# Both gates of a hybrid layer in the seven-product form, with weights summed and split once, ahead of time

## The chip, the cores and the metric

The kernel runs on one core of a Trainium2 chip. The metric is the device time of one execution in microseconds (us); of several runs the median is taken. TensorE (PE) does the matrix products, VectorE (DVE) and ScalarE (ACT) the element-wise work, GpSimd (POOL) a little, and SyncE (SP) issues nearly all transfers (DMAs), all from one queue that is worked off in order.

## The reference

One layer, D = 1024 channels, T = 2048 tokens, float32. What matters here is the frame around the mixer and its last two lines:

```python
def hybrid_layer(x, p_i, ...):
    h = rmsnorm(x, norm_pre)
    proj = h @ w_in
    # ... convolutions, chunked state-space scan (SSD), gates z -> y_ssd, y_sc
    mix = jnp.concatenate([y_ssd, y_sc], axis=-1) @ w_out
    x = x + rmsnorm(mix, norm_post)

    gate = jax.nn.sigmoid(x @ w_ple_gate)
    return x + gate * (p_i @ w_ple_proj)
```

The change concerns `x @ w_ple_gate`, a product of 2048 x 1024 by 1024 x 1024, called the gate below. The sigmoid is computed as half of 1 + tanh(half).

## The kernel before

**Numbers in two parts.** Every operand of a product is split into a high part (a cast on ACT to fp32r) and the remainder (a subtraction on DVE), and a product takes three matmuls (`PASSES`): high by high, high by low, low by high. `split_w` does it for a weight piece of 128 x 512 (four blocks of 128 x 128), `split_act` for an activation of 128 x 512 (L209 and L210 in the profile). One matmul is 128 x 128 by 128 x 512.

**Weights.** `Weights` holds the sequence of all weight pieces of the program in the order of their use. `W.next()` hands out the next one and starts the fetch of those that fit into six slots of 512 KB (`pw`, tag `wsp`, names `ws_...`). `direct` fetches a piece: a 256 KB load (L140) into one of nine raw buffers (`praw`, names `wr_...`), then the cast (L144) and the subtraction (L145) into the slot.

**Stages.** Channels are rows of 128, tokens are taken in groups of 512 (`tg` 0 to 3).

- Stage A, 0 to 1033 us: two blocks of 1024 tokens, the second one from 545 us. Each multiplies by `w_in` in 13 groups of two or one tiles, in a seven-product form: for a 2 x 2 arrangement of blocks, seven products of sums and differences of the blocks replace eight products (`Wino.multiply`, L316). The weight sums for it are made on DVE from raw pieces (`wino_pieces`, L184, L185, L187, L193). `multiply` takes a generator `meanwhile` and steps it after each of the seven products.
- The SSD scan to 1306 us, with half of the output projection under it.
- The rest of the output projection, `out_proj(0)` and `out_proj(2)` (products `mo`), to 1494.5 us; its results are the tiles `x2`.
- The gates. `gate_plain(0)` handles token groups 0 and 1: for each of 8 output rows and 2 groups, 24 matmuls `mg` (L220), 384 in all, with 16 raw pieces of `w_g`. `gate_seven(2)` handles groups 2 and 3: 28 pieces of 12 matmuls `mg_X`, `mg_Y` (L1259), 336 in all, in the order `GATES`; piece `(p, n)` is product p for output row pair n. Products 1, 5 and 6 are copied out of their bank, the others go to `finish` (tanh on ACT, three operations on DVE at most, a store).

**Order of the work.** All stages after the scan step through units (one unit is one `yield`): units 0 to 31 are the output projection, then 16 units of the plain gate and 28 of the other. `plan` says after which unit other work is written down: the norm of a token group (`second`, `norm`), the residual (`residual`, L1151 and L1152, with loads `xres`), the operands' split (`operands`, `operand`), the sums of gate weights (`gate_sums`: 16 loads, 16 sums, 16 stores to `sg_d`, L1192 to L1200), and the copy of `x2` into DRAM (`kept`), since `operand` overwrites it in groups 2 and 3; `finish` loads it again (`x<-x_d`). A scheduler turns the written order into each engine's order.

Of the kernel before, what the change touches and what calls it, by code (L numbers as in the profile page):

```python
# [64 lines left out]
def hybrid_kernel(ctx: ExitStack, tc: tile.TileContext, xT, pT, w_t, w_dt, w_o, w_g, w_p, cols_d, cst_d, outT):  # L65
# [1023 lines left out]
    with ExitStack() as st:  # L1089
# [64 lines left out]
        def operands(tg, d):  # L1154

            for i in range(2):
                sp_.setdefault(tg, []).append(split_act(x2s_[tg][d + i], f"x2s_{tg}_{d + i}", FIRST[2 * (tg % 2) + d // 4]))

        def gate_plain(t):

            for dp in range(0, KD, 2):
                sp = []
                for tg in (t, t + 1):
                    banks = pss.tile([P, 2, TG], F32, tag="ssd", name=f"mg_{tg}_{dp}")
                    for i in range(2):
                        d, ts_, ps = dp + i, slice(tg * TG, (tg + 1) * TG), banks[:, i, :]
                        pe = pp.tile([P, TG], F32, tag="pe", name=f"pe_{tg}_{d}")
                        nc.sync.dma_start(pe, ple_d[tg * TG // TB][d, :, tg * TG % TB:tg * TG % TB + TG])
                        for q in range(2):
                            if tg == t:  # L1170
                                sp.append(W.next(len(sp)))
                            mm3([(ps, sp[2 * i + q], sp_[tg])], 4 * q, 4, KD)
                        th = pp.tile([P, TG], F32, tag="gth", name=f"gth_{tg}_{d}")
                        S.activation(th, ps, AF.Tanh, scale=0.5)
                        V.scalar_tensor_tensor(th, th, 1.0, pe, ALU.add, ALU.mult)
                        V.scalar_tensor_tensor(th, th, 0.5, x2s_[tg][d], ALU.mult, ALU.add)
                        nc.sync.dma_start(outT[d, :, ts_], th)
                        yield

        def tmp(name):  # L1180
            return pp.tile([P, TG], F32, tag="x2", name=name, bufs=NG * KD)

        def kept(tg, d):
            for i in range(2):
                nc.sync.dma_start(x2_d[tg][d + i], x2s_[tg][d + i])

        def gate_sums(n):

            w = []
            for i, h in ((0, 0), (0, 1), (1, 0), (1, 1)):  # L1190
                w.append(tmp(f"sg_{n}_{i}{h}"))
                nc.sync.dma_start(w[-1].rearrange("p (k c) -> p k c", c=P), w_g[n + 4 * i, :, 4 * h:4 * h + 4, :])  # L1192
            yield
            a, b, c, d = w
            V.tensor_tensor(d, c, d, ALU.add)
            V.tensor_tensor(c, c, a, ALU.subtract)
            V.tensor_tensor(a, a, d, ALU.subtract)
            V.tensor_tensor(b, b, a, ALU.add)
            for i, v in enumerate((d, a, c, b)):
                nc.sync.dma_start(sg_d[n][i], v.rearrange("p (k c) -> p k c", c=P))  # L1200
            yield

        ops_ = {}

        def operand(g, k):

            p, t = GORDER[g], NG - 2
            b11, b12, b21, b22 = x2s_[t][k], x2s_[t + 1][k], x2s_[t][4 + k], x2s_[t + 1][4 + k]
            if p == 6:
# [4 lines left out]
            elif p == 7:
                src = b12
                V.tensor_tensor(b12, b12, b22, ALU.subtract)
            else:
                src = {1: b11, 2: b21, 5: b11, 3: b22, 4: b21}[p]
            ops_.setdefault(p, []).append(split_act(src, f"x2s_{p}{k}", FIRST[g % 4]))

        def gate_seven(t):
# [21 lines left out]
            for m, (p, n) in enumerate(GATES):  # L1243
                if m + 2 < len(GATES) and GATES[m + 2][1] % 2 == 0 and at(*GATES[m + 2]):
                    L.begin("pe", *at(*GATES[m + 2]))
                    L3.begin("x2", *at(*GATES[m + 2]))
# [10 lines left out]
                for k in range(4):  # L1257
                    for q, (a, b) in enumerate(PASSES):
                        TE.matmul(out, sp[:, a, k, :], ops_[p][k][:, b, :], start=p in OPENS and k == 0 and q == 0,  # L1259
# [36 lines left out]
        second(0, 16, (19, 20, 21, 22))  # L1296
        second(1, 18, (24, 25, 26, 27))
        for tg, units in ((0, (29, 29, 30, 30)), (1, (31, 31, 32, 32))):
            for n, u in enumerate(units):
                after(u, lambda tg=tg, d=2 * n: operands(tg, d))  # L1300
        second(2, 32, (34, 35, 36, 37))
        second(3, 34, (38, 39, 40, 41))
        for n in range(4):
            sums = gate_sums(n)
            for u in (36, 38):
                after(u + 2 * n, lambda sums=sums: next(sums))
        operands_at(0, 45, 46)
        operands_at(1, 46, 47)
        operands_at(2, 48, 49, 50, 51)
        operands_at(3, 52, 53)  # L1310
        operands_at(4, 54, 55)
        operands_at(5, 57, 59)
        operands_at(6, 61, 63)
# [70 lines left out]
```

## Time and profile before

| | us |
|---|---|
| three runs | 1675.41, 1677.62, 1675.29 |
| their median | 1675.41 |
| profiled execution | 1674.55 |
| its span | 1672.8 |
| granted TensorE clock, mean over the span | 0.997 of full speed |
| end of the output projection in it | 1494.5 |
| end of the last gate matmul in it | 1667.4 |

The span is the time from the first to the last instruction that the profiler saw; the execution's own time has 1.75 us around it. "Busy" is time in which an engine worked on an instruction. In the windows, each row gives a stretch, its length, the busy time of PE, PE's weight loads (PEld), DVE, ACT and POOL with the number of instructions, then the granted clock, the mean busy share of the 16 DMA engines and the rate in GB/s. In the waits, a row gives who waited for whom, the sum, the number of times and the longest. In the chain, a row is a piece of the path that ended last: start, length, engine and line. A row of the DMA issues gives the number of transfers, the size of one and the median time from issue to landing.

### The profile page before, as it was taken

Reading aid. Unit: us, or ns where it says so; the run is one execution under the profiler, and the core shown is the slowest. Engines: PE = TensorE matmul, PEld = TensorE weight load, DVE = VectorE, ACT = ScalarE, POOL = GpSimd, SP = SyncE. Lnnn points to the kernel's source line nnn. Section 1 sums busy time; section 2 is a strip of 40 time slices with the busy share of each in tenths; the row PEclk is TensorE's granted clock in tenths of the full one; section 3 lists DMA queues with packets and bytes.
Section 4 is the critical chain, followed back from the end, with each engine's and each line's share of the span. In section 5 each row is a group of like instructions: output and inputs, shape, how many; then the busy total and the mean of one; then the engine's idle time right before and its main releaser. Section 6 shows DMA issues by size and latency. Waiting matters only on the chain.

```text
span 1672.8 us, 22881 instructions
## 1 busy us (share of the span) xinstructions
PE 1647.1 (98%) x8352; PEld 1350.9 (81%) x8352; DVE 1278.3 (76%) x1909; ACT 800.0 (48%) x1442; POOL 45.6 (3%) x79
## 2 busy tenths in 40 slices
PE   9999999999999999999999999999999899999998
PEld 7888888888888888888888888877778688888776
DVE  5997777988669877677877677679878738768696
ACT  7763444434337434343444354566665424253363
POOL 0000000000000100100000001000000000000000
PEclk9999999999999999999999999999999999999999
DMA  8452322773226313221322237888888736537974
GB/s 300 160 195 80 100 95 77 260 252 110 65 65 218 134 64 109 77 82 63 107 70 103 69 102 245 257 297 273 283 299 249 251 110 208 194 118 264 307 259 151
DMA packets 132228, 281.15 MB, mean 168 GB/s; under 512 B 17930, under 2 KB 19466, under 8 KB 131092
## 3 DMA queue, kind: packets, MB, share of 16 engines
q1 hardware_dynamic: 132116, 279.70, 50.3%
q8 instruction: 65, 1.06, 0.3%
q14 instruction: 47, 0.39, 0.1%
HBM read 202.93 MB, written 76.72 MB: 167 GB/s over the span
## 4 chain that ended last, share of the span: by engine, by line
PE 87%; DMA 5%; DVE 4%; ACT 2%; issue 1%; SPq 1%; DVEq 0%; ACTq 0%
PE mo L220 9%; PE os L779 6%; PE mg L220 3%; PE mg_X L1259 3%; PE A_ple L220 3%; PE mg_Y L1259 2%; DMA mraw<-yz_d 2%; PE A_xs1X L316 1%; PE A_gc0X L316 1%; PE A_gc6X L316 1%; PE A_gb7X L316 1%; PE A_gb5X L316 1%; PE A_gc7X L316 1%; PE A_z3X L316 1%; PE A_xs3X L316 1%; PE A_gb6X L316 1%
## 5 line engine op out<-in xcount | busy, mean ns | idle before, releaser
L779 PE MATMUL os<-act_m,ws_os 128*128 128x512 f32 x768 | 184.3, 396 | 1.0 <-ACT A_z L714 0.7
L220 PE MATMUL mo<-act_m,ws_o 128*128 128x512 f32 x768 | 180.9, 394 | 4.5 <-DVE x L1115 1.8
L220 PEld LDWEIGHTS mo<-act_m,ws_o 128*128 128x128 f32 x768 | 142.6, 188 | 41.3 <-DVE x L1115 4.9
L779 PEld LDWEIGHTS os<-act_m,ws_os 128*128 128x128 f32 x768 | 142.2, 189 | 35.5 <-issue 4.6
L220 PE MATMUL mg<-act_x2s,ws_g 128*128 128x512 f32 x384 | 90.4, 394 | 3.3 <-ACT ws_g L144 3.3
L145 DVE TENSOR_TENSOR ws_A_gb<-wr_A_gb,ws_A_gb 128x512 fp32r<-128x512 f32 x96 | 66.0, 687 | 35.6 <-ACT ws_A_gb L144 35.5
L220 PEld LDWEIGHTS mg<-act_x2s,ws_g 128*128 128x128 f32 x384 | 71.3, 188 | 20.8 <-ACT ws_g L144 3.7
L144 ACT CAST ws_A_gc<-wr_A_gc 128x512 fp32r<-128x512 f32 x96 | 59.8, 623 | 57.8 <-PE A_gc5X L316 8.3
L144 ACT CAST ws_A_gb<-wr_A_gb 128x512 fp32r<-128x512 f32 x96 | 59.6, 621 | 54.8 <-PE A_cb0Y L316 4.3
L990 ACT ACTIVATE m<-m,adt 128x128 f32<-128x128 f32 x256 | 78.2, 391 | 7.9 <-DMA m<-acs_d 7.8
L633 DVE SCALAR_TENSOR_TENSOR xo<-ux,cols,xo 128x1024 f32<-128x1024 f32 x60 | 76.7, 1281 | 5.9 <-ACT xo L629 4.8
L145 DVE TENSOR_TENSOR ws_A_gc<-wr_A_gc,ws_A_gc 128x512 fp32r<-128x512 f32 x96 | 66.1, 688 | 14.4 <-ACT ws_A_gc L144 13.1
L209 ACT CAST act_m<-mraw 128x512 fp32r<-128x512 f32 x64 | 38.1, 621 | 31.7 <-DVE mraw L836 18.7
L144 ACT CAST ws_A_xs<-wr_A_xs 128x512 fp32r<-128x512 f32 x48 | 29.9, 622 | 44.7 <-issue 11.6
L993 DVE SCALAR_TENSOR_TENSOR m<-m,gsb 128x1024 f32<-128x1024 f32 x32 | 39.1, 1247 | 14.9 <-ACT m L990 13.3
L144 ACT CAST ws_A_z<-wr_A_z 128x512 fp32r<-128x512 f32 x48 | 29.9, 622 | 42.0 <-DVE wr_A_z L193 10.2
L145 DVE TENSOR_TENSOR ws_A_z<-wr_A_z,ws_A_z 128x512 fp32r<-128x512 f32 x48 | 33.0, 687 | 22.1 <-ACT ws_A_z L144 22.1
L220 PE MATMUL A_ple<-act_p,ws_p 128*128 128x512 f32 x192 | 48.3, 409 | 1.5 <-ACT act_p L209 1.0
L1115 DVE TENSOR_TENSOR x<-mo,part 128x512 f32<-128x512 f32 x32 | 22.0, 689 | 35.2 <-PE mo L220 33.9
L210 DVE TENSOR_TENSOR act_m<-mraw,act_m 128x512 fp32r<-128x512 f32 x64 | 41.8, 685 | 6.7 <-ACT act_m L209 6.4
L1259 PE MATMUL mg_X<-act_x2s,ws_g 128*128 128x512 f32 x192 | 45.6, 393 | 0.7 <-ACT gth L1230 0.7
L220 PEld LDWEIGHTS A_ple<-act_p,ws_p 128*128 128x128 f32 x192 | 36.7, 194 | 11.7 <-ACT act_p L209 1.9
(533 smaller groups left out, 3750.1 us busy)
## 6 DMA issues: line engine op xcount, KB each, us to landing
wr_A_gc<-in_w_t_dram SPq DMA_DIRECT2D x64, 256.0 KB, 2.6
wr_A_gb<-in_w_t_dram SPq DMA_DIRECT2D x64, 256.0 KB, 3.2
m<-acs_d SPq DMA_DIRECT2D x32, 512.0 KB, 8.3
ple_d<-A_pe SPq DMA_DIRECT2D x32, 256.0 KB, 3.5
wr_A_xs<-in_w_t_dram SPq DMA_DIRECT2D x32, 256.0 KB, 2.7
ysc_d<-vs SPq DMA_DIRECT2D x16, 512.0 KB, 2.7
wr_A_z<-in_w_t_dram SPq DMA_DIRECT2D x32, 256.0 KB, 2.6
xs_d<-xo SPq DMA_DIRECT2D x16, 512.0 KB, 2.8
```

The lines of the kernel that those rows point to most:

```text
L144: S.copy(sp[:, 0, :kn, :], raw[:, :kn, :])
L145: V.tensor_tensor(sp[:, 1, :kn, :], raw[:, :kn, :], sp[:, 0, :kn, :].bitcast(F32), ALU.subtract)
L209: S.copy(a[:, 0, :], src)
L210: V.tensor_tensor(a[:, 1, :], src, a[:, 0, :].bitcast(F32), ALU.subtract)
L220: TE.matmul(out, sp[:, a, (k0 + k) % 4, :], act[k0 + k][:, b, :], start=k0 + k == 0 and q == 0, stop=k0 + k == n - 1 and q == 2)
L316: TE.matmul(out, sp[:, a, k % 4, :], t[:, b, ts_], start=p in OPENS and k == 0 and q == 0, stop=k == nk - 1 and q == 2, skip_group_check=True)
L633: V.scalar_tensor_tensor(o, u[:, q:q + TB], col(w0 + q), o, ALU.mult, ALU.add)
L779: inst = f(*a, **k)
L990: S.activation(m[:, c, :], m[:, c, :], AF.Exp, bias=nacs[b][:, h, c:c + 1])
L993: V.scalar_tensor_tensor(mf, mf, 1.0, s["gsb"][gr], ALU.min, ALU.mult)
L1115: V.tensor_tensor(x2[d], ps[:, i, :], pt[:, i, :], ALU.add)
L1259: TE.matmul(out, sp[:, a, k, :], ops_[p][k][:, b, :], start=p in OPENS and k == 0 and q == 0, stop=k == 3 and q == 2, skip_group_check=True)
```

## The change

`gate_plain`, `operands`, `kept` and `gate_sums` go. `gate_weights` makes, for each of the four output row pairs n, all seven weight operands: four loads of 256 KB from `w_g`, four sums or differences, seven casts and seven subtractions, and seven stores of 512 KB (high and low part) into `sg_d[n]`. It runs as `meanwhile` of the second block of stage A, in groups 1 to 7 but the one that holds `cb`, up to seven steps after the seven products of a group. Both gates are `gate_seven`, for t = 0 and t = 2. Their weights come by `stored`: one 512 KB load from `sg_d` into the slot, with no cast and no subtraction. `operand` no longer overwrites `x2`: sums go to tiles of the raw pool `praw`, and `finish` reads `x2` where it is. The plan has other units, and `norm` a `lag` between its two steps.

```diff
-    sg_d = [dram.tile([4, P, 4, P], F32, name=f"sg_d{n}") for n in range(KD // 2)]
-    x2_d = {g: dram.tile([KD, P, TG], F32, name=f"x2_d{g}") for g in range(NG // 2, NG)}
+    sg_d = [dram.tile([7, P, 2, TG], F32, name=f"sg_d{n}") for n in range(KD // 2)]
...
+    def stored(src, name):
+
+        return name, lambda sp: nc.sync.dma_start(sp.bitcast(F32).rearrange("p a k c -> p a (k c)"), src)
...
-    seq += [direct(w_g[d, :, 4 * q:4 * q + 4, :], f"g0_{d}_{q}", praw) for d in range(KD) for q in (0, 1)]
...
-    seq += [direct(gate_piece(p, n), f"g2_{p}_{n}", praw) for p, n in GATES]
+    for t in range(0, NG, 2):
+        seq += [stored(sg_d[n][p - 1], f"g{t}_{p}_{n}") for p, n in GATES]
...
+        def gate_weights():
+
+            def loads(n):
+                w = []
+                for i, h in ((0, 0), (0, 1), (1, 1), (1, 0)):
+                    w.append(A.ph.tile([P, TG], F32, tag="h2", name=f"A_g{n}_{i}{h}"))
+                    nc.sync.dma_start(w[-1].rearrange("p (k c) -> p k c", c=P), w_g[n + 4 * i, :, 4 * h:4 * h + 4, :])
+                return w
+
+            for n in range(KD // 2):
+                a, b, d, c = loads(n)
+                yield
+                for p, src, op in ((1, a, None), (2, b, None), (4, d, None), (5, d, (c, d, ALU.add)),
+                                   (7, c, (c, a, ALU.subtract)), (6, a, (a, d, ALU.subtract)), (3, b, (b, a, ALU.add))):
+                    if op:
+                        V.tensor_tensor(src, *op)
+                    t = A.ph.tile([P, 2, TG], F32R, tag="h1", name=f"A_gs{n}_{p}")
+                    S.copy(t[:, 0, :], src)
+                    V.tensor_tensor(t[:, 1, :], src, t[:, 0, :].bitcast(F32), ALU.subtract)
+                    nc.sync.dma_start(sg_d[n][p - 1], t.bitcast(F32))
+                    yield
...
+            elif b and 0 < n < 8 and ("cb", 0) not in prs:
+                mean = (next(gw, None) for _ in range(7))
...
+            new = lambda: praw.tile([P, 4, P], F32, tag="wraw", name=f"t{p}_{t}{k}").rearrange("p k c -> p (k c)")
             if p == 6:
-                src = tmp(f"t2_{k}")
-                V.tensor_tensor(b11, b12, b11, ALU.subtract)
-                V.tensor_tensor(src, b11, b22, ALU.subtract)
-                V.tensor_tensor(b21, b21, src, ALU.add)
+                sums_[5, k] = new()
+                V.tensor_tensor(sums_[5, k], b12, b11, ALU.subtract)
+                src = sums_[6, k] = new()
+                V.tensor_tensor(src, sums_[5, k], b22, ALU.subtract)
...
-                V.scalar_tensor_tensor(th, th, 0.5, L3.get("x2", tg, d - i)[:, i, :], ALU.mult, ALU.add)
+                V.scalar_tensor_tensor(th, th, 0.5, x2s_[tg][d], ALU.mult, ALU.add)
...
-        for stage, t in ((out_proj, 0), (out_proj, 2), (gate_plain, 0), (gate_seven, 2)):
+        for stage, t in ((out_proj, 0), (out_proj, 2), (gate_seven, 0), (gate_seven, 2)):
```

What moves is seen in three places. In the rows below stand the line in the code, the operation, output and inputs, the shape, and how many stand together. On PE the order is the same up to the first gate matmul. There, before, right behind the output projection (names: `mg_0_0` is the bank of group 0, row 0; `ws_g0_0_1` the raw piece of row 0, half 1):

```order
L220 MATMUL mg_0_0_12674<-act_x2s_0_4_12621,ws_g0_0_1_12514 128x512 x3
L220 MATMUL mg_0_0_12674<-act_x2s_0_5_12624,ws_g0_0_1_12514 128x512 x3
L220 MATMUL mg_0_0_12674<-act_x2s_0_6_12627,ws_g0_0_1_12514 128x512 x3
L220 MATMUL mg_0_0_12674<-act_x2s_0_7_12630,ws_g0_0_1_12514 128x512 x3
L1131 MATMUL pn2_2_12738<-ones_d_102,ssq2_2_11974 128x1 x4
L220 MATMUL mg_1_0_12784<-act_x2s_1_0_12662,ws_g0_0_0_12509 128x512 x3
```

And now, at the same place of PE (`mg_0_X0` is the bank pair X of row pairs 0 and 1, `ws_g0_1_1` product 1 of row pair 1, `act_x2s_0_12` operand 1, part 2, of gate 0):

```order
L1236 MATMUL mg_0_X0_12814<-act_x2s_0_12_12767,ws_g0_1_0_12667 128x512 x3
L1236 MATMUL mg_0_X0_12814<-act_x2s_0_13_12770,ws_g0_1_0_12667 128x512 x3
L1151 MATMUL pn2_2_12847<-ones_d_100,ssq2_2_12132 128x1 x4
L1236 MATMUL mg_0_X2_12884<-act_x2s_0_10_12729,ws_g0_1_2_12815 128x512 x3
L1236 MATMUL mg_0_X0_12814<-act_x2s_0_10_12729,ws_g0_1_1_12669 128x512 x3
L1236 MATMUL mg_0_X0_12814<-act_x2s_0_11_12732,ws_g0_1_1_12669 128x512 x3
```

A piece is now used for 12 matmuls in a row, where one piece of before served 24, in two token groups.

On DVE, in the first group of stage A's second block, before (`ws_A1_gc0_3_0` is a split weight piece, product 3, of tile gc0 in block 1):

```order
L193 TENSOR_TENSOR wr_A1_gb0_000_4612<-wr_A1_gb0_010_4784,wr_A1_gb0_000_4612 128x512
L145 TENSOR_TENSOR ws_A1_gc0_3_0_4762<-wr_A1_gc0_000_4574,ws_A1_gc0_3_0_4762 128x512
L145 TENSOR_TENSOR ws_A1_gb0_3_0_4783<-wr_A1_gb0_000_4612,ws_A1_gb0_3_0_4783 128x512
L145 TENSOR_TENSOR ws_A1_gc0_7_0_4804<-wr_A1_gc0_100_4631,ws_A1_gc0_7_0_4804 128x512
L145 TENSOR_TENSOR ws_A1_gb0_7_0_4821<-wr_A1_gb0_100_4671,ws_A1_gb0_7_0_4821 128x512
L145 TENSOR_TENSOR ws_A1_gc0_2_0_4838<-wr_A1_gc0_010_4763,ws_A1_gc0_2_0_4838 128x512
L145 TENSOR_TENSOR ws_A1_gb0_2_0_4855<-wr_A1_gb0_010_4784,ws_A1_gb0_2_0_4855 128x512
```

And now (`A_gs0_1` is the split gate weight of product 1, row pair 0; `A_g0_11` a raw block of it):

```order
L196 TENSOR_TENSOR wr_A1_gb0_000_4610<-wr_A1_gb0_010_4782,wr_A1_gb0_000_4610 128x512
L549 TENSOR_TENSOR A_gs0_1_5108<-A_g0_00_5061,A_gs0_1_5108 128x512
L144 TENSOR_TENSOR ws_A1_gc0_3_0_4760<-wr_A1_gc0_000_4572,ws_A1_gc0_3_0_4760 128x512
L144 TENSOR_TENSOR ws_A1_gb0_3_0_4781<-wr_A1_gb0_000_4610,ws_A1_gb0_3_0_4781 128x512
L144 TENSOR_TENSOR ws_A1_gc0_7_0_4802<-wr_A1_gc0_100_4629,ws_A1_gc0_7_0_4802 128x512
L144 TENSOR_TENSOR ws_A1_gb0_7_0_4819<-wr_A1_gb0_100_4669,ws_A1_gb0_7_0_4819 128x512
L144 TENSOR_TENSOR ws_A1_gc0_2_0_4836<-wr_A1_gc0_010_4761,ws_A1_gc0_2_0_4836 128x512
L549 TENSOR_TENSOR A_gs0_2_5146<-A_g0_01_5063,A_gs0_2_5146 128x512
L549 TENSOR_TENSOR A_gs0_4_5182<-A_g0_11_5065,A_gs0_4_5182 128x512
L144 TENSOR_TENSOR ws_A1_gb0_2_0_4853<-wr_A1_gb0_010_4782,ws_A1_gb0_2_0_4853 128x512
L546 TENSOR_TENSOR A_g0_11_5065<-A_g0_10_5067,A_g0_11_5065 128x512
```

All 44 added operations of DVE stand in its rows 671 to 809, mixed with the splits, sums and evacuations of the block's first groups.

On SP's queue in the first gate, before (`wr_g...` raw pieces, `sg...` the weight sums, `pe` the embedding's projection):

```order
L1200 DMA sg_d2_94<-sg_2_01_13146 128x512
L1192 DMA sg_3_00_13231<-in_w_g_dram 128x512
L1192 DMA sg_3_01_13233<-in_w_g_dram 128x512
L1192 DMA sg_3_10_13235<-in_w_g_dram 128x512
L1192 DMA sg_3_11_13237<-in_w_g_dram 128x512
L1168 DMA pe_1_5_13239<-ple_d0_84 128x512
L1168 DMA pe_0_6_13271<-ple_d0_84 128x512
L140 DMA wr_g0_7_1_13279<-in_w_g_dram 128x512
```

And now, around the load of piece 5_2 (product 5, row pair 2):

```order
L151 DMA ws_g0_5_1_13058<-sg_d1_93 128x1024
L151 DMA ws_g0_3_0_13077<-sg_d0_92 128x1024
L1215 DMA out_0_dram<-kp_0_13_12929 128x512
L151 DMA ws_g0_3_1_13099<-sg_d1_93 128x1024
L840 DMA xres_3_2_13191<-in_xT_dram 128x2x512
L151 DMA ws_g0_5_2_13120<-sg_d2_94 128x1024
L840 DMA xres_3_4_13244<-in_xT_dram 128x2x512
L151 DMA ws_g0_5_3_13150<-sg_d3_95 128x1024
L151 DMA ws_g0_3_2_13171<-sg_d2_94 128x1024
```

The sums' loads and stores are gone from there; a weight is one transfer twice as large. On PE now, where 5_2 is used (`ws_g0_6_3` is the piece ahead of it in the written order, `mg_0_Y52` its bank):

```order
L1236 MATMUL mg_0_Y5_13149<-act_x2s_0_50_12844,ws_g0_5_0_13030 128x512 x3
L1236 MATMUL mg_0_Y5_13149<-act_x2s_0_51_12879,ws_g0_5_0_13030 128x512
L1236 MATMUL mg_0_X2_12884<-act_x2s_0_60_12841,ws_g0_6_3_13003 128x512 x3
L1236 MATMUL mg_0_X2_12884<-act_x2s_0_61_12876,ws_g0_6_3_13003 128x512 x3
L1236 MATMUL mg_0_X2_12884<-act_x2s_0_62_12905,ws_g0_6_3_13003 128x512 x3
L1236 MATMUL mg_0_X2_12884<-act_x2s_0_63_12935,ws_g0_6_3_13003 128x512 x3
L1236 MATMUL mg_0_Y5_13149<-act_x2s_0_51_12879,ws_g0_5_0_13030 128x512 x2
L1236 MATMUL mg_0_Y5_13149<-act_x2s_0_52_12908,ws_g0_5_0_13030 128x512 x3
L1236 MATMUL mg_0_Y5_13149<-act_x2s_0_53_12938,ws_g0_5_0_13030 128x512 x3
L1236 MATMUL mg_0_Y52_13248<-act_x2s_0_50_12844,ws_g0_5_2_13120 128x512 x3
L1236 MATMUL mg_0_Y52_13248<-act_x2s_0_51_12879,ws_g0_5_2_13120 128x512
L1236 MATMUL mg_0_Y5_13149<-act_x2s_0_50_12844,ws_g0_5_1_13058 128x512 x3
```

5_2 begins ahead of 5_1 and of 3_0 and 3_1, which SP loads before it: its first matmul stands 24 behind the last one of 6_2, whose slot it takes.

More of the change, by code (lines that the diff above doesn't have):

```diff
@@ L736, in hybrid_kernel @@
         v_ = {}
+        gw = gate_weights()
         first = first_input()
@@ L1122, in out_proj, with norm @@
                         yield
-        def norm(tg, unit):
+        def norm(tg, unit, lag):
             def sums():
@@ L1144, in norm @@
             after(unit, sums)
-            after(unit + 1, spread)
+            after(unit + lag, spread)
         def residual(tg, d):
@@ L1152, in residual @@
                 V.tensor_tensor(x2[d + i], x2[d + i], xk[:, i, :], ALU.add)
[L1154 to L1178, printed above, removed]
@@ L1180, in tmp @@
-        def tmp(name):
[L1181 to L1201, printed above, removed]
@@ L1203, in hybrid_kernel, with operand @@
-        ops_ = {}
-        def operand(g, k):
-            p, t = GORDER[g], NG - 2
+        def tmp(name):
+            return pp.tile([P, TG], F32, tag="x2", name=name, bufs=NG * KD + 4)
+        ops_, sums_ = {}, {}
+        def operand(t, g, k):
+            p = GORDER[g]
             b11, b12, b21, b22 = x2s_[t][k], x2s_[t + 1][k], x2s_[t][4 + k], x2s_[t + 1][4 + k]
+            new = lambda: praw.tile([P, 4, P], F32, tag="wraw", name=f"t{p}_{t}{k}").rearrange("p k c -> p (k c)")
             if p == 6:
-                src = tmp(f"t2_{k}")
-                V.tensor_tensor(b11, b12, b11, ALU.subtract)
-                V.tensor_tensor(src, b11, b22, ALU.subtract)
-                V.tensor_tensor(b21, b21, src, ALU.add)
+                sums_[5, k] = new()
+                V.tensor_tensor(sums_[5, k], b12, b11, ALU.subtract)
+                src = sums_[6, k] = new()
+                V.tensor_tensor(src, sums_[5, k], b22, ALU.subtract)
@@ L1214, in operand @@
             elif p == 7:
-                src = b12
-                V.tensor_tensor(b12, b12, b22, ALU.subtract)
-            else:
-                src = {1: b11, 2: b21, 5: b11, 3: b22, 4: b21}[p]
-            ops_.setdefault(p, []).append(split_act(src, f"x2s_{p}{k}", FIRST[g % 4]))
+                src = new()
+                V.tensor_tensor(src, b12, b22, ALU.subtract)
+            elif p == 4:
+                src = sums_[6, k]
+                V.tensor_tensor(src, b21, src, ALU.add)
+            else:
+                src = {1: b11, 2: b21, 5: sums_.get((5, k)), 3: b22}[p]
@@ L1221, in gate_seven @@
+            ops_.setdefault((t, p), []).append(split_act(src, f"x2s_{t}_{p}{k}", FIRST[(g + 7 * (t // 2)) % 4]))
         def gate_seven(t):
@@ L1258, in gate_seven @@
                     for q, (a, b) in enumerate(PASSES):
-                        TE.matmul(out, sp[:, a, k, :], ops_[p][k][:, b, :], start=p in OPENS and k == 0 and q == 0,
+                        TE.matmul(out, sp[:, a, k, :], ops_[t, p][k][:, b, :], start=p in OPENS and k == 0 and q == 0,
                                   stop=k == 3 and q == 2, skip_group_check=True)
@@ L1272, in after, with second, operands_at @@
             plan.setdefault(unit, []).extend(steps)
-        def second(tg, at_norm, at_res):
-            norm(tg, at_norm)
+        def second(tg, at_norm, at_res, lag):
+            norm(tg, at_norm, lag)
             for n, u in enumerate(at_res):
-                after(u - 1, lambda d=2 * n: L3.begin("xres", tg, d))
+                after(u - lag, lambda d=2 * n: L3.begin("xres", tg, d))
                 after(u, lambda d=2 * n: residual(tg, d))
-                if tg in x2_d:
-                    after(u + 1, lambda d=2 * n: kept(tg, d))
-        def operands_at(g, *units):
+        def operands_at(t, gs, *units):
             for k in range(4):
-                after(units[k * len(units) // 4], lambda k=k: operand(g, k))
+                for g in gs:
+                    after(units[k * len(units) // 4], lambda g=g, k=k: operand(t, g, k))
         def mixes_at(tg, *units):
@@ L1295, in hybrid_kernel @@
         mixes_at(3, 15, 15, 16, 17)
[L1296 to L1313, printed above, removed]
+        second(0, 16, (19, 20, 21, 22), 1)
+        second(1, 18, (24, 25, 26, 27), 1)
+        operands_at(0, (0,), 29, 30)
+        operands_at(0, (1,), 30, 31)
+        operands_at(0, (2, 3), 32, 33, 34, 35)
+        second(2, 32, (37, 39, 41, 43), 2)
+        operands_at(0, (4,), 37, 38, 39, 40)
+        second(3, 36, (45, 47, 49, 51), 2)
+        operands_at(0, (5,), 42, 43, 44, 45)
+        operands_at(0, (6,), 46, 48, 50, 52)
+        operands_at(2, (0,), 51, 52, 53, 54)
+        operands_at(2, (1,), 53, 54, 55, 56)
+        operands_at(2, (2,), 57, 58, 59, 60)
+        operands_at(2, (3,), 61, 62, 63, 64)
+        operands_at(2, (4,), 65, 66, 67, 68)
+        operands_at(2, (5,), 70, 71, 72, 73)
+        operands_at(2, (6,), 74, 75, 76, 77)
         for step in plan.get(-1, ()):
```

9 lines of the change are left out of this document (1 added, 8 removed).

## The prediction

> **What bounds the kernel now.** I read the page's totals first, then the windows by stage, the waits of TensorE (PE), the chain of waits at the end, and only then single instructions.
>
> ```profile
> span 1672.8 us, 22881 instructions
> PE 1647.1 (98%) x8352; PEld 1350.9 (81%) x8352; DVE 1278.3 (76%) x1909; ACT 800.0 (48%) x1442; POOL 45.6 (3%) x79
> ```
>
> The profiled execution took 1674.55 us, 1.75 us over its span and 0.86 us under the median of the runs (1675.41). PE is busy in 98% of the span, so only two things can shorten it: fewer matmuls, or less of the 25 us in which PE has none. The windows say the same of the two places that the change touches (the second block of stage A, 545 to 1033 us, and the gates, 1494.5 to 1667.4 us; the stretch 560 to 655 us is where the order puts the added work, beside DVE rows 671 to 809):
>
> ```profile
> core 0: us, PE busy (x) PEld busy (x) DVE busy (x) ACT busy (x) POOL busy (x), PEclk, DMA share, GB/s
> 545.00:1033.00 488.00, 487.32 (x2159) 403.21 (x2158) 367.84 (x530) 217.83 (x356) 21.76 (x22) 1.00 0.29 99
> 560.00:655.00 95.00, 95.00 (x421) 78.69 (x420) 66.74 (x99) 36.91 (x61) 1.66 (x3) 1.00 0.23 81
> 1494.50:1583.20 88.70, 85.42 (x378) 68.84 (x377) 61.52 (x101) 30.18 (x47) 0.00 (x0) 1.00 0.81 269
> 1515.00:1605.00 90.00, 86.72 (x376) 69.45 (x375) 71.47 (x117) 33.95 (x58) 0.00 (x0) 1.00 0.92 308
> 1583.20:1667.40 84.20, 83.47 (x360) 66.22 (x359) 71.82 (x114) 42.31 (x76) 0.00 (x0) 1.00 0.67 223
> 1667.40:1672.80 5.40, 0.00 (x0) 0.00 (x0) 1.39 (x2) 0.59 (x1) 0.00 (x0) 0.81 0.13 49
> ```
>
> Block 2 leaves PE idle for 0.7 us in 488. The gates leave it idle for 4 us; there the DMA engines are nearly full (share 0.92 at 308 GB/s for 90 us). Of the waits, two stand in the gates:
>
> ```profile
> PE mg L220 <- ACT ws_g L144: 3.3, 1, 3.3
> PE mg_X L1259 <- ACT gth L1230: 0.7, 1, 0.7
> ```
>
> The chain through the gates shows what the 3.3 us come from, and what a matmul costs:
>
> ```profile
> 1518.85 0.86 PE prs L1140 x2
> 1519.71 22.19 PE mg L220 x97
> ...
> 1552.79 0.63 SPq L1192
> ...
> 1554.68 5.34 DMA sg<-in_w_g_dram
> 1560.12 0.70 DVE sg L1195
> ...
> 1566.16 0.45 SPq L1200
> ...
> 1569.77 6.17 DMA wr_g<-in_w_g_dram
> 1576.02 0.63 ACT ws_g L144
> ...
> 1622.97 21.25 PE mg_Y L1259 x92
> 1644.23 19.45 PE mg_X L1259 x84
> ...
> 1667.40 0.60 ACT gth L1230
> ```
>
> SP's one queue holds the loads and stores of the weight sums (L1192, L1200); a raw weight piece for the plain gate is issued behind them, takes 6.17 us, is split, and PE waits. A plain gate matmul is 22.19/97 = 0.2288 us, one of the seven-product gate 21.25/92 = 0.2310 or 19.45/84 = 0.2315.
>
> **The change, part by part.**
>
> 1. *First gate in seven products.* The plain gate has 384 matmuls (2 token groups, 8 output pieces, 24 each), the seven-product one 28 pieces of 12, 336. The 48 that go are 11.0 us at 0.2288. If the new ones run at the 0.2315 of the last gate, it is 384 x 0.2288 - 336 x 0.2315 = 10.1 us. I take -10.5.
>
> 2. *The stall of 3.3 us goes* with what makes it: after has no sums, no raw load and no split of gate weights in this stage. -3.3. The 0.7 us wait for the last bank stays, as does the tail of 5.4 us after the last matmul.
>
> 3. *Weights come split, 512 KB a piece, straight into the six slots.* What is late next: SP issues a load when its slot's earlier piece is done, and PE needs it five pieces later (5 x 12 x 0.231 = 13.9 us) where pieces are used in the order loaded. At one place they aren't: piece 5_2 takes the slot of 6_2, and PE reaches it 24 matmuls, 5.5 us, after 6_2 ends. No row loads 512 KB of presplit weights; the nearest are other 512 KB loads in the gates, and a 256 KB one for the bottom:
>
> ```profile
> xres<-in_xT_dram SPq DMA_DIRECT2D x6, 512.0 KB, 5.7
> wr_g<-in_w_g_dram SPq DMA_DIRECT2D x11, 256.0 KB, 3.9
> wr_g<-sg_d SPq DMA_DIRECT2D x9, 256.0 KB, 5.8
> x<-x_d SPq DMA_DIRECT2D x3, 512.0 KB, 5.9
> ```
>
> With 5.7 to 5.9 us and 0.5 us of SP's issue (the 0.45 above) it is 0.7 to 0.9 us late, once in each gate; at 3.9 it isn't late at all. 5_2 also holds xres, 5_3 and 3_2 behind it in SP's queue, which have 8 us or more to spare. I take +2.0 for both gates with a bank wait of some 0.3; bounds 0 and 8 (rival 1). [...]
>
> 4. *Traffic in the gates.* Out go 44 raw loads, 16 loads and 16 stores of the sums, and 16 stores (256 KB) and 8 loads (512 KB) of x2: 28.3 MB. In come 56 loads of 512 KB: 29.4 MB. From the last output matmul on I count 21.8 MB for the first gate (74 us with what lies on PE beside its matmuls: 295 GB/s) and 23 MB for the second (299 over 77 us). That is below the 308 that was held for 90 us, but not by much. Zero here; the price of less is rival 1.
>
> 5. *DVE, ACT in the first gate.* DVE gets 44 operand operations, 32 of the residual, 12 additions of products and 32 at the outputs: 120. An operation takes 0.69 us in the rows but starts every 0.60 when nothing waits:
>
> ```profile
> 545.25 0.69 DVE L184 TENSOR_TENSOR wr_A_gb_e<-wr_A_gb,wr_A_gb 128x512 f32<-128x512 f32 x1 [0.15 <-DMA wr_A_gb<-in_w_t_dram]
> 545.86 0.68 DVE L686 TENSOR_TENSOR us<-A_gc7X,A_gc 128x512 f32<-128x512 f32 x1
> 546.46 0.68 DVE L185 TENSOR_TENSOR wr_A_gb<-wr_A_gb,wr_A_gb 128x512 f32<-128x512 f32 x1
> 565.91 0.69 DVE L184 TENSOR_TENSOR wr_A_gc_e<-wr_A_gc,wr_A_gc 128x512 f32<-128x512 f32 x1 [2.31 <-DMA wr_A_gc<-in_w_t_dram]
> L144 ACT CAST ws_g<-wr_g 128x512 fp32r<-128x512 f32 x41 | 25.4, 620 | 29.6 <-DMA wr_g<-in_w_g_dram 7.4 <-issue 6.0 <-PE mg L220 5.2
> ```
>
> 120 x 0.60 = 72 us of 77: full, but in the order an operand stands 18 to 20 us of PE work ahead of its first matmul. Cover gone, a slip of DVE by more than that shows; 0 taken.
>
> 6. *Weight sums and splits under stage A.* Added: 16 loads (4.2 MB), 16 sums and 28 subtractions on DVE (44 x 0.60 = 26.4 us), 28 casts on ACT (28 x 0.62 = 17.4), 28 stores (14.7 MB), 44 issues on SP (44 x 0.6 = 26 us of its queue). They land in 560 to 655. DVE there: 66.7 + 26.4 = 93.1 of 95 us; ACT 36.9 + 17.4 = 54.3; DMA 81 + 18.9 MB/95 us = 280 GB/s. Nothing of these is bound, but DVE has no slack in the first 95 us and then only catches up (367.8 busy of 488 in the whole block). A product's evacuation or a weight's split may come up to 2 us later; banks and slots leave 8 to 13 us by the order. PE pays only beyond that. Not below nothing, since PE idles only 0.7 us in this block; above, 26.4 less the 28.3 us that DVE is idle leaves under 2, and with the 2.31 us of a DMA wait like the one at 565.91 some 4. I take +0.5, near the lower end, as the row of 560 to 655 shows PE never short while DVE idles for 28 us.
>
> Sum: -10.5 - 3.3 + 2.0 + 0 + 0 + 0.5 = -11.3. 1674.55 - 11.3 = 1663.25 for the profiled execution; +0.86 for the median, and rounded, **1664.0**.
>
> **Rivals.**
>
> 1. *The gates become DMA bound.* For it: share 0.92 before, and a 512 KB piece every 2.77 us is 189 GB/s of weights alone, twice the bytes that a raw piece had. Against: the bytes in all hardly rise. If 283 GB/s is what they get, 21.8 MB takes 77 us and 23 MB 81.3, +3 and +4, in place of the +2.0: 1669.
>
> 2. *DVE overfull under block 2.* For it: 93 of 95. Against: 0.60 a piece with the queue full, the order's margins, and less DVE work after 655. If every third added operation (15 x 0.60 = 9 us) reached PE less the bank's slack, +5 to +7: 1669 to 1671.
>
> 3. *The other side: slower.* The DMA rate in the gates falls under 254 GB/s: 44.8 MB then take more than 176.3 us, against 172.9 from the first gate matmul to the last before, and the time is 1678.8 or more. For it: the first gate had only 269 by the windows, with SP waiting in between. Against: 308 for 90 us in the same stage with smaller transfers.
>
> 4. *No new stall:* 512 KB land within 5 us and stage A gives nothing: 1675.41 - 13.8 = 1661.6; with 0.2267 a matmul, as in block 2, another 3: 1659.
>
> ```profile
> 545.20 2.88 PE L316 MATMUL A_gc0X<-act_A,ws_A_gc 128*128 128x512 f32 x12
> 547.92 1.30 PE L316 MATMUL A_gb0X<-act_A,ws_A_gb 128*128 128x512 f32 x5
> ```
>
> (From 545.20 to 547.92 are 2.72 us for 12.)
>
> **How the numbers follow.** A forecast within some 3 us of the sum has 0.5, rival 4 0.15, rival 1 0.2, rival 2 0.1, rival 3 0.05. The range reaches from rival 4's 1659.5 to 1670.5, most of rivals 1 and 2. A measurement tells 0.2%, 3.35 us: faster is under 1672.1. Rivals 1 and 2 could run on past it, so faster 0.88, same 0.06, slower 0.06.
>
> **What the profile of the changed kernel would show.** 8304 matmuls; no wait of mg for ws_g by ACT. Step 3 is right if PE waits for ws_g by a DMA, about 1 us at 5_2 in each gate, and wrong if such waits come at many pieces (rival 1) or none (rival 4). Step 6 is right if block 2 ends within 1 us of 1033 and PE's waits there stay under 1 us; if waits for DVE lines of the product sums or splits appear between 560 and 700, it is rival 2. Step 5 is wrong if PE waits for act_x2s. The forecast fails if 512 KB loads in the gates take over 8 us in the median.

## The result and the profile after

| | before | after |
|---|---|---|
| median, us | 1675.35 (6 runs) | 1663.66 (6 runs, 1661.37 to 1668.13) |
| ratio | | 0.993, 95% interval 0.9916 to 0.9945 |
| profiled execution, us | 1674.55 | 1662.03 |
| its span, us | 1672.8 | 1660.3 |

The change makes the kernel faster by 0.7%. The forecast was 1664.0, in a range of 1659.5 to 1670.5. The page of the changed kernel:

```profile
span 1660.3 us, 22845 instructions
PE 1637.5 (99%) x8304; PEld 1343.2 (81%) x8304; DVE 1288.3 (78%) x1933; ACT 797.4 (48%) x1446; POOL 64.5 (4%) x79
```

There are 48 matmuls fewer. The windows of the changed kernel (columns as before: stretch, length, busy time of PE, PEld, DVE, ACT, POOL, granted clock, DMA share, GB/s):

```profile
545.00:1033.00 488.00, 487.33 (x2159) 403.26 (x2158) 390.90 (x573) 230.28 (x383) 39.85 (x22) 1.00 0.40 135
560.00:655.00 95.00, 95.00 (x420) 78.70 (x420) 87.92 (x141) 47.60 (x85) 18.29 (x4) 1.00 0.74 258
1494.50:1572.00 77.50, 76.26 (x336) 60.74 (x335) 72.22 (x120) 33.52 (x58) 0.00 (x0) 1.00 0.87 286
1572.00:1655.00 83.00, 82.13 (x355) 65.28 (x353) 45.73 (x71) 27.19 (x47) 0.00 (x0) 1.00 0.80 275
1515.00:1605.00 90.00, 88.76 (x383) 70.56 (x383) 77.82 (x126) 38.13 (x66) 0.00 (x0) 1.00 0.93 312
```

Under stage A, DVE went from 66.7 to 87.9 busy us of 95 and the transfers from 81 to 258 GB/s, and PE still has no idle time there. PE's waits in the gates are these:

```profile
PE mg_Y L1236 <- DMA ws_g<-sg_d: 1.0, 1, 1.0
PE mg_X L1236 <- ACT gth L1208: 0.7, 1, 0.7
PE mg_X L1236 <- DVE kp L1210: 0.3, 1, 0.3
```

The timeline of PE (start, length, work, and in brackets the idle time before it) says where the gates begin and end; first the last 24 projection matmuls, then the first gate matmuls behind them, the piece after the DMA wait, and the last piece:

```profile
1488.89 5.74 PE L223 MATMUL mo<-act_m,ws_o 128*128 128x512 f32 x24
1494.46 1.98 PE L1236 MATMUL mg_X<-act_x2s,ws_g 128*128 128x512 f32 x8
...
1534.11 19.66 PE L1236 MATMUL mg_Y<-act_x2s,ws_g 128*128 128x512 f32 x84 [0.97 <-DMA ws_g<-sg_d]
...
1651.80 3.01 PE L1236 MATMUL mg_X<-act_x2s,ws_g 128*128 128x512 f32 x12 [0.69 <-ACT gth L1208]
```

The chain of waits shows what the 0.97 us are: a 6.34 us load of a gate weight, issued when a slot came free, with products of the pieces around it before and after.

```profile
1520.24 7.37 PE mg_X L1236 x32
1527.61 0.02 issue
1527.63 6.34 DMA ws_g<-sg_d
1533.97 0.14 issue
1534.11 16.96 PE mg_Y L1236 x72
```

**The account.** Gate matmuls behind the projection run from 1494.46 to 1654.81 us, 160.35; before it was 1494.35 to 1667.36, 173.0. Less the waits (1.93 now, 3.95 before) and the 3.3 us of `pn` and `prs`, 668 matmuls take 155.1 us (0.2322 each) where 716 took 165.75 (0.2315; four are ahead of the projection's end in both). That is -10.6 for the matmuls, -3.3 for the stall, +1.2 for new waits, and +0.1 for all that lies before. Together -12.6; the spans differ by 12.5.

### The profile page after: what moved, and what is told of

Its sections match the earlier page's. It is cut to its first block, busy times and chain, and to the rows that moved or that the text cites. A ratio compares the mean times of both kernels' runs of the same rounds, so it can differ in the third digit from the quotient of the medians.

```text
span 1660.3 us, 22845 instructions
## 1 busy us (share of the span) xinstructions
PE 1637.5 (99%) x8304; PEld 1343.2 (81%) x8304; DVE 1288.3 (78%) x1933; ACT 797.4 (48%) x1446; POOL 64.5 (4%) x79
## 4 chain that ended last, share of the span: by engine, by line
PE 87%; DMA 5%; DVE 5%; ACT 2%; issue 1%; SPq 0%; DVEq 0%; ACTq 0%
PE mo L223 8%; PE os L801 6%; PE mg_X L1236 5%; PE mg_Y L1236 4%; PE A_ple L223 3%; DMA mraw<-yz_d 2%; PE A_xs1X L319 1%; PE A_gc0X L319 1%; PE A_gc6X L319 1%; PE A_gb5X L319 1%; PE A_gb7X L319 1%; PE A_gb4X L319 1%; PE A_z2X L319 1%; PE A_xs0X L319 1%; PE A_cb0X L319 1%; PE A_z3X L319 1%
## 5 line engine op out<-in xcount | busy, mean ns | idle before, releaser
L1236 PE MATMUL mg_X<-act_x2s,ws_g 128*128 128x512 f32 x384 | 91.5, 395 | 1.0 <-ACT gth L1208 0.7
L1236 PEld LDWEIGHTS mg_X<-act_x2s,ws_g 128*128 128x128 f32 x384 | 70.9, 188 | 19.7 <-ACT kp L1240 1.8
L1236 PE MATMUL mg_Y<-act_x2s,ws_g 128*128 128x512 f32 x288 | 68.2, 393 | 1.0 <-DMA ws_g<-sg_d 1.0
L1236 PEld LDWEIGHTS mg_Y<-act_x2s,ws_g 128*128 128x128 f32 x288 | 53.4, 188 | 14.1 <-issue 1.4
L1140 ACT ACTIVATE sq<-x 128x512 f32<-128x512 f32 x28 | 17.7, 632 | 64.8 <-DVE x L1135 64.5
```

The lines of the kernel that those rows point to most:

```text
L1236: TE.matmul(out, sp[:, a, k, :], ops_[t, p][k][:, b, :], start=p in OPENS and k == 0 and q == 0, stop=k == 3 and q == 2, skip_group_check= ...
```

## The experiments

The whole runs of one kernel spread by 2 to 10 us here, so a term of 1 us is read from the profiles, as a length: from the start of the last 24 projection matmuls to the end of the last gate matmul, called the gate length below. It is 1667.36 - 1488.74 = 178.6 us before and 1654.81 - 1488.89 = 165.9 after.

### Is the work under stage A free?

The kernel before, with `gate_weights` added and its results stored aside:

```diff
+    sgx_d = [dram.tile([7, P, 2, TG], F32, name=f"sgx_d{n}") for n in range(KD // 2)]
...
+                    nc.sync.dma_start(sgx_d[n][p - 1], t.bitcast(F32))
...
+            elif b and 0 < n < 8 and ("cb", 0) not in prs:
+                mean = (next(gw, None) for _ in range(7))
```

> The kernel before, with the changed kernel's weight sums and splits added under the second block of stage A and stored to a DRAM tensor that nothing reads; the gates are those of before. If that work is free (theory: DVE has 28 us of idle time in 560 to 655, banks and slots cover 8 to 13 us of lag), the time is that of before, ratio 0.9995 to 1.0005, and PE stays idle for under 1 us in 545 to 1033. If it is paid for under PE (rival 2 of the prediction), 5 to 7 us more, ratio 1.003 to 1.004, with PE waits in 560 to 700.

Measured: 1676.9 against 1676.47 us, ratio 1.0003 (0.9991 to 1.0015). Block 2 in its profile:

```profile
545.00:1033.00 488.00, 487.33 (x2159) 403.27 (x2158) 390.90 (x574) 229.72 (x382) 38.66 (x22) 1.00 0.40 134
```

PE's 487.33 us of 488 are those of before. It is free, and rival 2 is out at this size.

How much more would go there was asked by doing each of the 28 subtractions of the changed kernel three times:

```diff
-                    V.tensor_tensor(t[:, 1, :], src, t[:, 0, :].bitcast(F32), ALU.subtract)
+                    for _ in range(3):
+                        V.tensor_tensor(t[:, 1, :], src, t[:, 0, :].bitcast(F32), ALU.subtract)
```

> The changed kernel with each of the 28 subtractions under stage A done three times: 56 more DVE operations, 34 us at 0.60, in the same rows. DVE was busy 88 of 95 us from 560 to 655, so some 27 us don't fit. Theory of a margin of 8 to 13 us: PE waits for what is beyond it, 10 to 18 us more than the changed kernel (1674 to 1682), with waits for splits or evacuations between 600 and 700. Rival: the margin is far larger (the lag is taken up later, where DVE idles), and it costs under 2 us.

Measured: 1663.11 us, ratio 0.992 (0.9907 to 0.9933), as the changed kernel. In the profile the last added subtraction starts at 747.6 us in place of 653.4, DVE is busy for 184 us of the 188 from 560 to 748, and PE waits in this block for 1.35 us more than nothing:

```profile
L550 DVE TENSOR_TENSOR A_gs<-A_g,A_gs x84: 681/685/692, 557.3 to 747.6; 128x512 fp32r<-128x512 f32 x84
560.00:748.00 188.00, 186.65 (x823) 153.91 (x822) 184.06 (x284) 89.04 (x153) 28.19 (x11) 1.00 0.52 178
PE A_cb0X L319 <- DVE ux L640: 1.1, 1, 1.1
PE A_cb0X L319 <- ACT A_cb L323: 0.2, 1, 0.2
```

The rival's price held: 34 us of further DVE work cost 1.35 us of PE. It does not measure the margin of 8 to 13 us, which I had read from banks and slots. The added work did not stay in the same rows, as the text above has it: it is spread over 190 us in place of 94, among later work of the block, so it is mostly the added work itself that got late. How far the block's own splits and evacuations can lag isn't shown.

### What does the first gate's form give by itself?

The kernel before, with the plain first gate kept and only the second gate's weights made under stage A (the sums leave the gates; `gate_weights` and `stored`, not printed here, are those of the changed kernel):

```diff
-    seq += [direct(gate_piece(p, n), f"g2_{p}_{n}", praw) for p, n in GATES]
+    seq += [stored(sg_d[n][p - 1], f"g2_{p}_{n}") for p, n in GATES]
...
-        for n in range(4):
-            sums = gate_sums(n)
-            for u in (36, 38):
-                after(u + 2 * n, lambda sums=sums: next(sums))
```

> The plain first gate kept (384 matmuls, raw pieces split in place), the second gate's weights made under stage A and loaded split; the sums' 32 transfers and 16 additions are gone from the gates. Theory: the 48 matmuls stay (10.5 us), the 3.3 us stall goes, since the sums held SP's queue: 1672 to 1673, ratio 0.998 to 0.9985, 8352 matmuls, no wait of mg for ws_g by ACT of over 1 us. Rival: the stall is that of a raw load in a full DMA stage and stays: 1675, ratio 1.000.

Measured: 1672.89 against 1676.47 us, ratio 0.9974 (0.9965 to 0.9984). Its page and its waits in the gates:

```profile
PE 1649.2 (99%) x8352; PEld 1353.2 (81%) x8352; DVE 1275.9 (76%) x1909; ACT 798.6 (48%) x1442; POOL 63.3 (4%) x79
PE mg_X L1267 <- ACT gth L1238: 0.7, 1, 0.7
1515.00:1605.00 90.00, 90.00 (x397) 72.81 (x396) 66.87 (x107) 31.84 (x52) 0.00 (x0) 1.00 0.73 238
```

The wait for `ws_g` is gone with the sums, and the DMA rate of the middle 90 us fell from 308 to 238 GB/s: with the chain of before, in which the late raw load stands behind the sums' transfers, this puts the stall down to the sums, as step 2 had it. The splits of the second gate's weights left the gates too, and whether the sums' place in SP's queue or their bytes made the load late isn't taken apart. The gate length is 1667.07 - 1492.52 = 174.6 us, 4.1 less than before; the changed kernel's 165.9 is another 8.6 less. The stall alone is 3.3 and the 48 matmuls less the new waits are 9.4, so 0.8 us of the first step are not accounted for.

### What makes the DMA wait at 5_2?

The changed kernel with the pieces in another order:

```diff
-         + [(p, n) for h in (0, 2) for p in (5, 3) for n in (h, h + 1)]
+         + [(5, 0), (5, 2), (5, 1), (3, 0), (3, 1), (5, 3), (3, 2), (3, 3)]
```

> The changed kernel with products 5 and 3 in the order 5_0 5_2 5_1 3_0 3_1 5_3 3_2 3_3, in loads and products, so that no piece is used less than 32 matmuls (7.4 us) after its slot is free. Theory: the 0.97 us wait for ws_g by a DMA at 5_2 is made by the slot, and goes: 1 us less than the changed kernel (ratio to before about 0.9925), no wait of PE for a DMA in the gates. Rival: the DMA engines are the limit there and the wait turns up at another piece: no gain.

Measured: 1662.49 us, ratio 0.9919 (0.9902 to 0.9935). The gate length is 1657.34 - 1492.31 = 165.0 us; PE's waits in the gates:

```profile
PE mg_X L1236 <- ACT gth L1208: 0.7, 1, 0.7
PE mg_Y L1236 <- DVE kp L1210: 0.6, 1, 0.6
PE mg_X L1236 <- DVE kp L1210: 0.3, 1, 0.3
```

The wait for a DMA is gone, and 0.6 us of a wait for DVE came in. A second profile was to tell it from chance:

> The kernel with 5_2 ahead of 5_1 unchanged, for a second profile. Theory: from the last 24 projection matmuls to the last gate matmul it takes 165.0 us within 0.3 (165.9 and 166.5 in the two profiles of the changed kernel), with no wait for a DMA. Rival: the DMA wait is a matter of chance and comes back at some piece.

Its gate length is 1655.71 - 1490.64 = 165.1 us, again with no wait for a DMA. The changed kernel was profiled again as well:

> The changed kernel unchanged, as the yardstick for the three that run with it. Its runs spread from 1661.4 to 1668.1. Theory: the spread comes from ahead of the gates (the scan and the output projection, where the end of the projection was 1494.5 in one profile and 1497.9 in another of a near relative), and the gates from the last projection unit on take the 165.9 us of the first profile within 0.5. Rival: the spread is of the gates, which sit near the DMA limit, and a profile of another time shows it there.

Measured: 1662.4 us, ratio 0.9922 (0.9909 to 0.9935). This profiled execution took 1666.17 us, and the rows of its timeline say why:

```profile
1492.48 5.74 PE L223 MATMUL mo<-act_m,ws_o 128*128 128x512 f32 x24
...
1538.22 19.67 PE L1236 MATMUL mg_Y<-act_x2s,ws_g 128*128 128x512 f32 x84 [1.52 <-DMA ws_g<-sg_d]
...
1655.94 3.01 PE L1236 MATMUL mg_X<-act_x2s,ws_g 128*128 128x512 f32 x12 [0.69 <-ACT gth L1208]
```

The last projection unit starts 3.6 us later than in the first profile (1488.89); the gate length is 166.5, 0.55 us longer, which is the wait at 5_2 (1.52 against 0.97). So most of the 4.1 us between the two profiles arises ahead of the gates, in work that the change leaves alone. The order with 5_2 first gains 0.9 to 1.4 us by the gate length and is the best version here, though whole runs can't tell it from the changed kernel.

### Are the gates near a DMA limit?

One kernel with less traffic: `pe` is loaded once and used for all outputs, so the embedding's part of the output is another.

```diff
-                    L.begin("pe", *at(*GATES[m + 2]))
+                    L.begin("pe", 0, 0)
...
-                V.scalar_tensor_tensor(th, th, 1.0, L.get("pe", tg, d - i)[:, i, :], ALU.add, ALU.mult)
+                V.scalar_tensor_tensor(th, th, 1.0, L.get("pe", 0, 0)[:, i, :], ALU.add, ALU.mult)
```

> The changed kernel with the gates' pe loaded once for all (15 of 16 loads of 512 KB left out, 7.9 MB of some 45 in the gates). If only the slot at 5_2 costs, a lighter DMA stage lands 5_2 in time, and the time is 1 us less than the changed kernel's. Rival 1 of the prediction, in part (the gates are DMA bound over some of their length): 3 us less or more.

Measured: 1663.66 us, ratio 0.9936 (0.992 to 0.9951); by whole runs that is 1.3 us more than the changed kernel run beside it, not 1 less. The gate length is 1655.76 - 1491.02 = 164.7 us, 1.2 to 1.7 less, and the only waits of PE left there are the two that aren't for a DMA:

```profile
1515.00:1605.00 90.00, 89.69 (x389) 71.52 (x388) 79.31 (x129) 38.20 (x65) 0.00 (x0) 1.00 0.82 264
PE mg_X L1236 <- ACT gth L1208: 0.7, 1, 0.7
PE mg_X L1236 <- DVE kp L1210: 0.3, 1, 0.3
```

7.9 MB less in the gates give what the wait at 5_2 took, and little more. Two kernels with more:

```diff
...
+                if m % 2 == 0:
+                    nc.sync.dma_start(more_d[t // 2][m // 2], x2s_[t][m // 4])
```

> The changed kernel with 28 stores of 256 KB to a DRAM tensor that nothing reads, one at every second piece of both gates: 52.1 MB in place of 44.8 over 160 us, 326 GB/s. Theory: the DMA engines give 312 GB/s over a long stretch (the changed kernel's row of 1515 to 1605), so the gates become DMA bound and take 167 us: 7 us more than the changed kernel, with PE waits for ws_g by DMA at many pieces. Rival: they give the 332 that a full share would be, and it costs under 2 us.

Measured: 1665.18 us, ratio 0.9936 (0.9923 to 0.9948), 2.8 us over the changed kernel run beside it. In the profile the gate length is 1655.45 - 1490.08 = 165.4 us, not longer than without the stores, and no wait for `ws_g` is left. But the scheduler did not leave one store at every second piece: 14 of the 28 are issued by 1437 us, under the output projection, four in the first gate and ten in the second. The windows of the gates:

```profile
1494.50:1572.00 77.50, 76.99 (x339) 61.47 (x338) 73.03 (x121) 34.37 (x58) 0.00 (x0) 1.00 0.89 299
1572.00:1655.00 83.00, 82.21 (x356) 65.52 (x355) 46.07 (x71) 27.33 (x46) 0.00 (x0) 1.00 0.92 310
```

With a store at every piece (no `if`):

> As the run with 28 more stores, now 56 of 256 KB, one at every piece of both gates: 59.5 MB over 160 us would be 372 GB/s, above any row of this case. The 28 stores cost nothing and reached 318 GB/s. Theory: the ceiling is near 332 GB/s (the full share): 59.5 MB take 179 us, 15 to 19 us more than the changed kernel, with PE waits for ws_g by DMA throughout. Rival: the gates still fit (SP's queue runs far enough ahead, and the ceiling is nearer 370): under 5 us more.

Measured: 1669.67 us, ratio 0.9961 (0.9948 to 0.9973). Its gate length is 1663.13 - 1495.78 = 167.4 us, 0.9 to 1.4 more than the changed kernel; PE waits for a gate weight once. Here 28 of the 56 stores are issued ahead of the gates (the first row), again four in the first gate, 23 in the second, and one behind the last matmul:

```profile
more_d<-x SPq DMA_DIRECT2D x28, 256.0 KB, 5.6
PE mg_Y L1238 <- DMA ws_g<-sg_d: 0.4, 1, 0.4
1573.00:1663.10 90.10, 88.05 (x380) 69.72 (x378) 50.54 (x79) 28.87 (x49) 0.00 (x0) 1.00 0.96 340
1630.00:1650.00 20.00, 20.00 (x89) 16.16 (x88) 11.64 (x18) 4.85 (x8) 0.00 (x0) 1.00 1.02 358
```

Both my theories of a ceiling missed, and neither experiment is as strong as its text: 3.7 and 7.1 MB went in while the gates ran, not 7.3 and 14.7. What they show is that the second gate takes 340 GB/s over 90 us, and 358 over 20, with no wait of PE that the profile puts down to a transfer. The first gate was hardly loaded more (317 GB/s from 1515 to 1605, against 312 in the changed kernel), so how near it is to a limit stays open.

The whole runs of these two kernels lost 2.8 us, and by the ratios 6.5 (0.9961 against 0.9922), both over the 2 and 5 us that the rivals allowed. Most of it is not in the gate length. Under the output projection, where the other half of the stores went, PE waits longer for DVE to empty the banks of `mo`, in the changed kernel first, then in the one with 56 stores:

```profile
PE mo L223 <- DVE x L1135: 0.5, 2, 0.3
PE mo L224 <- DVE x L1136: 3.1, 5, 1.5
```

With 28 stores it is 3.4 us. DVE itself waits there for the loads `xres`, 5.7 us with 56 stores in place of 0.6, which points at loads delayed by the stores; that wasn't tried by itself. The store behind the last matmul goes with a tail of 6.9 us (5.5 in the changed kernel).

### Does DVE bound the first gate?

The changed kernel with the subtraction of each gate operand done twice:

```diff
-            ops_.setdefault((t, p), []).append(split_act(...))
+            a = split_act(...)
+            V.tensor_tensor(a[:, 1, :], src, a[:, 0, :].bitcast(F32), ALU.subtract)
+            ops_.setdefault((t, p), []).append(a)
```

> The changed kernel with the subtraction of each gate operand done twice: 28 more DVE operations a gate, as many as splitting the weights in the gates would take. The first gate then has 148 x 0.60 = 89 us of DVE work in 77. Theory: the operands stand 18 to 20 us ahead of PE, which covers the 12 us, and DVE catches up in the second gate: under 2 us more than the changed kernel. Rival: DVE bounds the first gate: 8 to 12 us more, with PE waiting for act_x2s.

Measured: 1665.26 us, ratio 0.9938 (0.9926 to 0.9951), 2.9 us over the changed kernel run beside it; the gate length is 1660.57 - 1491.18 = 169.4, 2.9 to 3.5 more. Its waits and windows:

```profile
PE mg_X L1238 <- DVE kp L1212: 3.9, 2, 2.4
PE mg_Y L1238 <- DMA ws_g<-sg_d: 1.6, 2, 1.3
1515.00:1605.00 90.00, 84.83 (x367) 67.84 (x367) 86.91 (x143) 33.69 (x59) 0.00 (x0) 1.00 0.89 294
```

Between theory and rival. PE does not wait for `act_x2s`: the operands' lead covers the lag, as step 5 said. It waits for L1212, the addition that empties a product's bank, which has no such lead: by the code, product 4 is added into the bank that product 7 has just been read from. The scheduler also put some pieces of products 7 and 4 in another order in this kernel, and PE waits 1.6 us for gate weights here, so not all of the 3 us need be DVE's.

## Why the prediction was right, point by point

1. *48 matmuls, -10.5.* Measured -10.6. The matmuls of both gates now take 0.2322 us in the mean, like those of the last gate before (0.2310 to 0.2315), not at the 0.2267 of stage A.
2. *The stall, -3.3.* It went. That the sums made it is shown by the chain of before and by the kernel that takes them out of the gates, with the second gate's splits beside them.
3. *+2.0 for late weights.* This term was too large: 1.24 us in one profile (0.97 at 5_2, 0.27 for a bank), 1.8 in the other (1.52 and 0.28). The mechanism was as written, slot and 24 matmuls; another order of the pieces removes it. But it was forecast at 0.7 to 0.9 us in each gate, and it came in the first gate alone, and larger: two errors that offset each other in part. There 5_2's load took 6.3 us, against 5.7 to 5.9 in the forecast; in the second, with 303 GB/s around it, loads landed in 4.6 in the median, as the rows of the DMA issues in a window at each place show (the first holds one load, the second five):

```profile
ws_g<-sg_d SPq DMA_DIRECT2D x1, 512.0 KB, 6.3
ws_g<-sg_d SPq DMA_DIRECT2D x5, 512.0 KB, 4.6
```

4. *Traffic, 0.* Right: apart from 5_2, PE waits for no transfer in the gates. Rivals 1 and 3 were priced with a ceiling of 254 to 308 GB/s. 308 was what this stage asked for, not what the engines could give, since the second gate took 340 over 90 us. For the first gate, whose 312 GB/s was never raised beyond 318, that is not shown.
5. *DVE in the first gate, 0.* Right at 72 us of 77, with 0.27 us of waits for L1210. Its cover was named only in part: 17 us more cost some 3 us, most of it at the bank and none at the operand.
6. *Stage A, +0.5.* Measured 0.1 at most in the profile, and 1.0003 by itself. The reason given, a margin of 8 to 13 us, was not put to the test: with three times the subtractions the added work was itself what got late, up to 748 us, and its first result is loaded again at 1470.

The sum was -11.3 for the profiled execution and came to -12.5: the terms of steps 3 and 6 were about 1.2 too high. The median was met more closely than that, 1663.66 against 1664.0, since the first profile of the changed kernel is 1.6 us under the median of its runs, where the one before was 0.86 under: chance, not insight.

## What to carry to other kernels

Where PE is busy for 98% of the span, count matmuls and stalls first; in this case work for other engines was nearly free in a stage where PE idles for 0.7 us of 488, even with DVE near full: 23 us more of DVE's busy time cost PE nothing, another 34 us cost it 1.35, and what got late was mostly the moved work itself. A rate of transfers seen in a busy stage need not be the limit (here 308 GB/s over 90 us before, and 340 over 90 us with the added stores); before it is used as one, add traffic, see in the order of the queue that it lands in the stage in question, and then whether PE waits. For loads into a ring of slots, compare the landing time under load with the matmuls between the freeing of each slot and its next use: here one piece out of order made the only such wait of the changed kernel (0.97 and 1.52 us in two profiles, none with another order).

## What the hardware showed unexpectedly

The stall that the change removes could have cost more than its length. In the kernel with stage A's work added to the one before, the same stall was 3.60 us in place of 3.26, and the 26 matmuls behind it took 7.84 us in place of 6.50, and the granted clock, the third figure from the end in the windows' rows, fell to 0.50 (before, the rows from 1570 to 1590 all have 1.00). Before first, then with the work added:

```profile
1576.69 6.50 PE L220 MATMUL mg<-act_x2s,ws_g 128*128 128x512 f32 x26 [3.26 <-ACT ws_g L144]
1578.07 7.84 PE L221 MATMUL mg<-act_x2s,ws_g 128*128 128x512 f32 x26 [3.60 <-ACT ws_g L145]
1578.00:1580.00 2.00, 1.93 (x7) 1.56 (x8) 2.00 (x5) 1.26 (x3) 0.00 (x0) 0.78 0.82 305
1580.00:1582.00 2.00, 2.00 (x6) 1.62 (x5) 2.00 (x4) 0.72 (x2) 0.00 (x0) 0.50 0.79 216
```

So 0.34 us more of waiting came with 1.7 us more in all. These two stalls alone would fit a bound between 3.26 and 3.60 us of waiting, but other rows don't: in the kernel before, the clock fell to 0.50 within 1.4 us behind a wait of 2.37, and behind the last matmul it was at 0.50 from at most 2.05 us on in one profile and still full after 5.03 us in another. Below are that wait and its clock, then the tails of the second profile of the changed kernel (last matmul to 1658.95) and of the kernel with doubled operand subtractions (to 1660.57):

```profile
1246.62 2.85 PE L779 MATMUL pst<-xdd,btok 128*64 128x128 f32 x30 [2.37 <-DVE xdd L943]
1248.00:1249.00 1.00, 1.00 (x11) 1.00 (x10) 0.71 (x2) 1.00 (x5) 0.00 (x0) 0.50 0.99 406
1661.00:1662.00 1.00, 0.00 (x0) 0.00 (x0) 0.04 (x1) 0.00 (x0) 0.00 (x0) 0.50 0.10 37
1664.60:1665.60 1.00, 0.00 (x0) 0.00 (x0) 0.00 (x0) 0.00 (x0) 0.00 (x0) 1.00 0.00 0
```

So in these rows the length of a stall does not tell by itself whether the clock falls; what else decides it, no run here takes apart.

GpSimd's three copies of 128 x 2 under stage A took 5.97 us in the mean in place of 2.16 (from 545 to 700 us, before first, then after), beside a fuller DVE. By the timeline they are 11.33, 6.00 and 0.58 us in place of 5.30, 0.58 and 0.58, and DVE has no gap while the two long ones run. Nothing waited for them. The copy of 11.33 us runs beside 20 DVE operations, that of 6.00 beside 11; why the copies get longer, no run here takes apart.

```profile
L685 POOL COPY us<-halo_s 128x2 f32<-128x2 f32 x3 | 6.5, 2158 | 79.0 <-DVE xo L635 47.9 <-DVE A_z L665 26.9 <-DVE vs L694 4.3
L704 POOL COPY us<-halo_s 128x2 f32<-128x2 f32 x3 | 17.9, 5972 | 67.5 <-DVE xo L654 42.3 <-DVE A_z L684 22.1 <-DVE vs L713 3.1
```
